# A conv block on one core: one tile's copies moved behind a sigmoid, four subtractions moved from VectorE to POOL

## The chip, the cores and the metric

The kernel runs on one core of one Trainium2 chip. The metric is the device time of one execution in microseconds (us), as a median of several runs. Engines are named as in the profile: PE (TensorE, matmuls) with PEld (its weight loads), DVE (VectorE), ACT (ScalarE), POOL (GpSimd) and SP (SyncE, which here only issues DMAs).

## The reference

One decoder layer on 256 tokens of width 2048, in float32, with a modulation by a condition vector `c`. The layer's mixer is a gated depthwise convolution of 31 taps; the attention mixers of the reference are not used at depth 1.

```python
mod = silu(c) @ mod_w + mod_b
sh1, sc1, g1, sh2, sc2, g2 = split(mod, 6)
h = rms_norm(x, norm1_g) * (1 + sc1) + sh1
a, gt = split(h @ conv_w_in + conv_b_in, 2)
u = a * sigmoid(gt)
u = causal_depthwise_conv(u, conv_dw_w, 31 taps) + conv_dw_b
u = silu(layer_norm(u, conv_ln_g, conv_ln_b))
y = u @ conv_w_out + conv_b_out
x = x + (1 + g1) * y
h = rms_norm(x, norm2_g) * (1 + sc2) + sh2
u = square(relu(h @ mlp_w1))
x = x + (1 + g2) * (u @ mlp_w2)
```

## The kernel before

**Tiles.** Activations lie with channels on the 128 partitions: 16 channel tiles of 128 x 256 tokens. Weights come from HBM as tiles of 1 MB (128 x 2048, `raw`, five buffers, loaded in the order of a written list by SP). To keep float32 accuracy, each weights tile is split in two halves of 128 x 1024, and each half into a high part and a low part: `hi` is a copy by ACT (L203), `lo` is the difference `raw - hi` by VectorE or POOL (L206). Both have six buffers. PE multiplies hi and lo with the split activations (`hl`, `u2`).

**Stages, in order of time.**

1. Start (to about 138 us): the modulation's columns are formed on VectorE (L381, one multiply and sum over 128 x 2048 for each 1 MB column tile `mod_c`), the first norm is made, and PE multiplies the first eight pairs of the input projection in plain float32 into eight held accumulators (L550).
2. Input projection, jobs 8 to 15: each job has two weights tiles, `("in", i, 0)` for `a` and `("in", i, 1)` for the gate. The result goes through `evac` (L506, L507) and `gate` (a sigmoid on ACT, L738, and a product on VectorE, L740) into `u[i]`. Beside it run the convolutions. Eight channel tiles are convolved on VectorE, tap by tap (L609 to L618). The other eight (`PE_TILES`) go to PE (L723): for these ACT or VectorE first makes sixteen shifted copies of `u[i]` into a tile `wide` (`copy_wide`, L700), and POOL makes a diagonal matrix (L708). `COPY_AT` tells at which job the copies of which tile are put: at job 8 those of tile 0. PE also multiplies the remaining modulation rows (L307) between the jobs.
3. The first `gate` calls are for the eight held accumulators, `held[0]` to `held[7]`. They share the code place with the split of job 8's two weights tiles:

```python
split_w(jobs[HELD] + (0,), nc.gpsimd)
with tc.issue_after(state["w_hi"]):
    gate(0, held[0])
for i in range(1, 6):
    gate(i, held[i])
with tc.issue_after(state["sg"].ins):
    split_w(jobs[HELD] + (1,), nc.gpsimd)
with tc.issue_after(state["w_hi"]):
    gate(6, held[6])
gate(7, held[7])
```

4. Layer norm of the convolved tiles (from about 300 us), with silu.
5. Output projection, eight pairs `("out", 0)` to `("out", 7)` (about 309 to 411 us). The prediction calls these jobs 0 to 7 of the output stage. Each has two weights tiles, so four halves to split; a pair's result is scaled by ACT (L904) and added to the residual `x` by VectorE (L905), then ACT squares it (L907), POOL sums the squares into `sqacc` (L909, L912), and ACT and VectorE split the scaled result (L916, L214, L217). Sixteen more columns of the modulation are formed on VectorE beside it (L381).
6. The MLP in four quarters (to the end).

**Order.** A scheduler sorts each engine's instructions by priorities and by a planned time of its own; `urgent()` raises a priority, and `tc.issue_after(x)` puts what is inside behind the instruction `x`. Each engine then works off its own list in that order. `state["sg"]` is the sigmoid of the last `gate` call made so far.

**Who makes the low parts.** All of the input projection's are made by POOL (but for one half of job 8). For the pairs in the list `POOLED` they are made by POOL as well; all other pairs' are made by VectorE.

## Time and profile before

| What | us |
|---|---|
| Median of 3 runs | 1118.45 |
| Lowest and highest run | 1117.72, 1119.9 |
| The profiled execution, its own time | 1120.38 |
| Span of the profiled execution, first to last instruction | 1118.6 |
| PE busy in that span | 1092.7 |
| DVE, ACT, POOL busy | 761.7, 506.6, 164.9 |

The profile is of one execution. A row of its timeline has start and duration in us, engine, line, operation, output and inputs by the program's names, partitions x elements, how many instructions are merged, and in brackets the engine's idle time before it and what ended it. A table of stretches has, for each engine, its busy time in the stretch, then the clock that was granted to PE as a share of full speed, the share of time that the DMA engines were busy, and what they moved.

### The profile page before, as it was taken

The page shows a single profiled execution, that of the slowest core. Times are in us where ns is not written, and L with a number is a line of the kernel's source. Part 1 is how long each engine was busy: PE and PEld are TensorE (multiplying, and loading weights), DVE is VectorE, ACT ScalarE, POOL GpSimd, SP SyncE. Part 2 cuts the span into 40 slices and gives each one's busy share as a digit, 9 for nine tenths or more (in the row PEclk, how much of TensorE's full clock was granted, in tenths as well). Part 3 has the DMA queues.
Part 4 walks back from the last instruction along what each step waited for, and adds up shares of the span by engine and source line. Part 5 has one row for each costly group of instructions (what it writes and reads, how often), then busy time and mean ns, then how long its engine had stood idle before and what let it go on. Part 6 is the DMA issues. An engine that isn't in the chain of part 4 may idle for free.

```text
span 1118.6 us, 15367 instructions
## 1 busy us (share of the span) xinstructions
PE 1092.7 (98%) x6018; PEld 897.3 (80%) x6018; DVE 761.7 (68%) x1018; ACT 506.6 (45%) x675; POOL 164.9 (15%) x102
## 2 busy tenths in 40 slices
PE   7999989999999999999999999999999999999998
PEld 4887856766789988888888888888888888888887
DVE  5777679798399977676776567644656566565553
ACT  4111284673566568444344444334444433444441
POOL 0000175657443434000000000000000000000000
PEclk8999989999999989999999999999999999999999
DMA  9999977998489977798898889758788877788641
GB/s 384 420 421 421 416 283 308 406 326 309 145 345 358 387 252 264 233 285 268 337 368 310 249 235 305 271 180 260 229 249 240 230 207 223 217 253 248 212 142 38
DMA packets 142314, 314.22 MB, mean 281 GB/s; under 512 B 87585, under 2 KB 105505, under 8 KB 107297
## 3 DMA queue, kind: packets, MB, share of 16 engines
q1 hardware_dynamic: 142096, 313.11, 80.7%
q8 instruction: 47, 0.77, 0.3%
q14 instruction: 25, 0.20, 0.0%
q10 hardware_dynamic: 146, 0.13, 0.0%
HBM read 301.15 MB, written 12.07 MB: 280 GB/s over the span
## 4 chain that ended last, share of the span: by engine, by line
PE 78%; DMA 12%; DVE 6%; ACT 2%; issue 2%; POOL 1%; ACTq 0%; SPq 0%; POOLq 0%; DVEq 0%
PE mm L255 20%; PE mm L254 20%; PE mm L256 20%; DMA raw<-mod_c 8%; PE mm L231 4%; PE mm L227 3%; PE mm L229 3%; PE mm L228 2%; DVE raw L381 2%; DMA raw<-w_in 2%; PE mm L232 2%; DVE acc L615 2%; PE row L307 1%; DMA raw<-w_out 1%; ACT wide L700 1%
## 5 line engine op out<-in xcount | busy, mean ns | idle before, releaser
L203 ACT ACTIVATE hi<-raw 128x1024 fp32r<-128x1024 f32 x320 | 334.7, 1057 | 371.7 <-PE mm L256 297.3
L206 DVE TENSOR_TENSOR lo<-raw,hi 128x1024 fp32r<-128x1024 f32 x273 | 335.7, 1238 | 175.3 <-ACT hi L203 173.2
L255 PE MATMUL mm<-lo,u 128*128 128x512 f32 x496 | 193.1, 389 | 0.0
L254 PE MATMUL mm<-hi,u 128*128 128x512 f32 x496 | 193.0, 389 | 0.0
L256 PE MATMUL mm<-hi,u 128*128 128x512 f32 x496 | 192.9, 389 | 0.0
L254 PE MATMUL mm<-hi,hl 128*128 128x512 f32 x480 | 186.7, 389 | 0.0
L256 PE MATMUL mm<-hi,hl 128*128 128x512 f32 x480 | 186.7, 389 | 0.0
L255 PE MATMUL mm<-lo,hl 128*128 128x512 f32 x480 | 186.7, 389 | 0.0
L381 DVE SCALAR_TENSOR_TENSOR raw<-raw,cond 128x2048 f32<-128x2048 f32 x62 | 146.1, 2363 | 50.5 <-DMA raw<-mod_c 50.3
L206 POOL TENSOR_TENSOR lo<-raw,hi 128x1024 fp32r<-128x1024 f32 x47 | 114.5, 2459 | 216.0 <-DMA raw<-w_in 132.4
L256 PEld LDWEIGHTS mm<-hi,u 128*128 128x128 f32 x496 | 93.1, 188 | 19.4
L255 PEld LDWEIGHTS mm<-lo,u 128*128 128x128 f32 x496 | 93.1, 188 | 19.3 <-DVE lo L206 0.4
L254 PEld LDWEIGHTS mm<-hi,u 128*128 128x128 f32 x496 | 93.1, 188 | 19.0
L256 PEld LDWEIGHTS mm<-hi,hl 128*128 128x128 f32 x480 | 90.1, 188 | 18.8
L254 PEld LDWEIGHTS mm<-hi,hl 128*128 128x128 f32 x480 | 90.1, 188 | 18.7
L255 PEld LDWEIGHTS mm<-lo,hl 128*128 128x128 f32 x480 | 90.1, 188 | 18.6
L615 DVE SCALAR_TENSOR_TENSOR acc<-u,v,acc 128x256 f32<-128x256 f32 x224 | 94.6, 488 | 1.8
L227 PE MATMUL mm<-hl,hi 128*128 128x256 f32 x288 | 82.7, 289 | 4.4 <-ACT hi L203 2.2
L231 PE MATMUL mm<-hl,hi 128*128 128x512 f32 x224 | 83.7, 412 | 3.0 <-ACT hi L203 2.2
L229 PE MATMUL mm<-hl,lo 128*128 128x256 f32 x288 | 82.8, 288 | 0.6 <-DVE lo L206 0.6
L228 PE MATMUL mm<-hl,hi 128*128 128x256 f32 x288 | 82.7, 288 | 0.2 <-DVE hl L217 0.2
L550 PE MATMUL mm<-two,first 128*128 128x256 f32 x256 | 60.7, 392 | 8.5 <-ACT two L581 8.5
(170 smaller groups left out, 1193.9 us busy)
## 6 DMA issues: line engine op xcount, KB each, us to landing
raw<-w SPq DMA_DIRECT2D x128, 1024.0 KB, 5.3
raw<-mod_c SPq DMA_DIRECT2D x62, 1024.0 KB, 9.2
raw<-mod_r SPq DMA_DIRECT2D x32, 1024.0 KB, 7.7
raw<-w_in SPq DMA_DIRECT2D x16, 1024.0 KB, 6.9
raw<-w_out SPq DMA_DIRECT2D x16, 1024.0 KB, 6.4
first<-w_first SPq DMA_DIRECT2D x15, 1024.0 KB, 17.2
flat<-two SPq DMA_DIRECT2D x30, 256.0 KB, 2.7
two<-flat SPq DMA_DIRECT2D x120, 64.0 KB, 4.3
```

Source lines behind the costliest of these rows:

```text
L203: state["w_hi"] = nc.scalar.activation(hi, w[:, ks, :], AF.Copy).ins
L206: end = by.tensor_tensor(lo, w[:, ks, :], hi.bitcast(F32), op=ALU.subtract)
L227: nc.tensor.matmul(out_p, w, m[:, 0:T], start=begin, stop=False)
L228: nc.tensor.matmul(out_p, w, m[:, T : 2 * T], start=False, stop=False)
L229: state["mm_end"] = nc.tensor.matmul(out_p, lo[:, k % HALF, :], m[:, 0:T], start=False, stop=end)
L231: nc.tensor.matmul(p[:, c, :], hi[:, k % HALF, :], m, start=(k == 0), stop=(k == KT - 1))
L254: nc.tensor.matmul(p, p_hi, hi, start=begin, stop=False)
L255: nc.tensor.matmul(p, p_hi, lo, start=False, stop=False)
L256: nc.tensor.matmul(p, p_lo, hi, start=False, stop=end)
L381: nc.vector.scalar_tensor_tensor(w, w, 1.0, cb, op0=ALU.mult, op1=ALU.mult, accum_out=acc)
L550: step = nc.tensor.matmul(held[n][:, c, :], w[:, 2 * n + c, :], h, start=k == 0 and c == 0, stop=k == KT - 1, skip_group_check=True)
L615: nc.vector.scalar_tensor_tensor(out, s, w, acc, op0=ALU.mult, op1=ALU.add)
```

## The change

Two edits. In the list of pairs whose low parts are made by POOL, `("out", 2)` is added. And the call that makes the shifted copies of tile 0 (at job 8, which equals `HELD`) is put inside `issue_after`, behind the sigmoid of the last `gate` call, that of `held[7]`; the other calls of `copy_wide` stay as they are.

```diff
-POOLED = [("out", 0), ("out", 1), ("up", 0, 1), ("up", 0, 2)]
+POOLED = [("out", 0), ("out", 1), ("out", 2), ("up", 0, 1), ("up", 0, 2)]
...
         if n in COPY_AT:
-            copy_wide(COPY_AT[n], False)
+            with tc.issue_after(state["sg"].ins) if n == HELD else ExitStack():
+                copy_wide(COPY_AT[n], False)
```

Both edits also move other instructions, since the scheduler plans anew. In the changed program's lists: ACT has sigmoids 3 to 5 and the hi halves of job 8's second tile ahead of all copies of tile 0; ten of the copies come after sigmoid 7, then the hi halves of job 9's first tile, then the last six. Further on, the two instructions that make the shift of the convolution (L658) stand ahead of the four hi halves of job 12 instead of between them. In the output stage POOL has four lows of `("out", 2)` between those of `("out", 1)` and the first sum of squares, and VectorE's L905 of pair 0 comes directly after an L381, no longer behind three of these lows. SP issues the same loads in the same order; some of them wait for a slot that POOL frees where it was VectorE or PE before.

## The prediction

> **What bounds the kernel now.** I read the page of the profile first (busy shares, the granted clock in slices, the chain), then tables of busy time by stretch.

> ```profile
> PE 1092.7 (98%) x6018; PEld 897.3 (80%) x6018; DVE 761.7 (68%) x1018; ACT 506.6 (45%) x675; POOL 164.9 (15%) x102
> PEclk8999989999999989999999999999999999999999
> PE 78%; DMA 12%; DVE 6%; ACT 2%; issue 2%; POOL 1%; ACTq 0%; SPq 0%; POOLq 0%; DVEq 0%
> 440.00:1118.00 678.00, 674.75 (x3021) 560.11 (x3019) 421.97 (x445) 279.10 (x286) 0.25 (x1) 1.00 0.77 242
> ```

> PE is busy 98% of the span and makes 78% of the chain. From 440 us on it has 674.75 of 678 us busy at full clock, so whatever PE gains or loses before 440 comes out at the end unchanged. The question is where PE stands still or runs slowly before 440. The clock line has two tenths under 9 there, the sixth and the fifteenth slice (about 140 to 168 and 391 to 420 us). Narrow stretches (PE alone) show both places, and a third for comparison:

> ```profile
> 143.09:146.50 3.41, 0.72 (x3) 1.00 0.35 147
> 146.50:153.33 6.83, 5.42 (x16) 0.50 0.32 95
> 306.93:310.35 3.42, 1.95 (x18) 1.00 1.04 441
> 392.26:395.68 3.42, 1.25 (x11) 1.00 0.97 376
> 395.68:402.50 6.82, 6.27 (x28) 0.50 0.92 315
> ```

> Columns: stretch, length, busy PE, granted clock, DMA share. At 143 us PE is idle 2.69 us of 3.41, then gets half clock for 6.83 us. At 392 us it is idle 2.17 us of 3.42, again with half clock for 6.82 us behind. At 307 us it is idle 1.47 us and the clock stays. So in this trace an idle share between 1.47 and 2.17 us of such a stretch is where the penalty begins. [...]

> The change touches the first place and the stage ahead of the second.

> **Edit 1, the copies behind the last sigmoid.** ACT, then PE and POOL, then the load concerned and PE's last matmuls of the held groups:

> ```profile
> 135.12 0.84 ACT L738 ACTIVATE two<-mm,v 128x256 f32<-128x256 f32 x2 [0.56 <-DVE u L740]
> 137.85 5.40 ACT L700 ACTIVATE wide<-u 32x284 f32<-32x284 f32 x12 [1.89 <-issue]
> 143.65 0.83 ACT L738 ACTIVATE two<-acc,v 128x256 f32<-128x256 f32 x2
> 144.36 2.01 ACT L203 ACTIVATE hi<-raw 128x1024 fp32r<-128x1024 f32 x2
> 145.47 0.49 PE L231 MATMUL mm<-hl,hi 128*128 128x512 f32 x1 [2.16 <-ACT hi L203]
> 147.91 0.58 PE L232 MATMUL mm<-hl,lo 128*128 128x256 f32 x1 [1.94 <-POOL lo L206]
> 145.50 14.07 POOL L206 TENSOR_TENSOR lo<-raw,hi 128x1024 fp32r<-128x1024 f32 x6 [7.25 <-ACT hi L203]
> 124.64 2.88 SPq L184 DMA_DIRECT2D raw<-w_in  x3
> raw<-w_in SPq DMA_DIRECT2D x1, 1024.0 KB, 11.5
> 134.15 1.89 PE L550 MATMUL acc<-two,first 128*128 128x256 f32 x8
> 136.74 1.03 PE L550 MATMUL row<-two,first 128*128 128x256 f32 x4
> 137.41 0.59 PE L231 MATMUL mm<-hl,hi 128*128 128x512 f32 x1
> 143.04 0.28 PE L232 MATMUL mm<-hl,lo 128*128 128x256 f32 x1
> ```

> After three sigmoids ACT's queue holds twelve copies of the shifted tile. They wait until PE has finished the start stage (137.77) and then run to 143.25. Queued behind them are the sigmoids 3 to 7 and the two hi halves of job 8's second weights tile, whose load had landed at 124.64 + 11.5 = 136.1. PE waits 2.16 us for that hi, 1.94 us for its low part on POOL.

> In the changed program's order ACT has sigmoids 3 to 5 next, then the two hi halves, sigmoids 6 and 7, and only then copies. Acc's matmuls end at 136.04, so three sigmoids at 0.42 us (0.84 for two) end by about 137.8 even if the first waits for VectorE's last gate product. The hi halves (2.01 for two) end by 138.9 and 139.8, and POOL's lows, 14.07 / 6 = 2.35 us each, at about 141.3 and 143.7. PE comes to them at 143.3 and needs the second half three us later: no wait, with 2 us to spare. Gained: idle 2.69 + (6.83 - 5.42) = 4.10 us, and half of the 5.42 us at half clock, 2.71. Together 6.8 us.

> What comes late next? The copies move behind: ten from about 141, then the hi halves of job 9's first tile to 147.5, its lows at 149.0 and 151.4. PE took 5.9 us for job 8's first tile (137.41 to 143.32), so it ends the second near 149; a group of row matmuls lies between, so job 9 starts about 150 with its first low there. The next tile's lows are due 154.1 and 156.5, ahead of PE by 3 us. The copies themselves feed a convolution that PE begins only after job 9. Loads on SP's queue wait for slots that POOL's lows and PE's row matmuls free; both come earlier, and the DMA engines have room:

> ```profile
> 143.50:154.30 10.80, 6.88 (x25) 4.65 (x25) 10.52 (x27) 10.65 (x19) 8.80 (x4) 0.68 0.36 125
> 211.28 0.88 DVE L613 SCALAR_TENSOR_TENSOR acc<-u,v,small 128x256 f32<-128x256 f32 x2 [8.04 <-ACT shift L658]
> 239.28 0.47 PE L231 MATMUL mm<-hl,hi 128*128 128x512 f32 x1 [0.56 <-DVE u L740]
> ```

> The DMA share is 0.36 there. VectorE's taps could have taken the gain back later, since PE waits 0.56 us for VectorE at 239. But VectorE itself had stood 8.04 us waiting for ACT's shift, and the new order puts both shift instructions ahead of four hi halves that stood before or between them. I take the 0.56 us as gone too. Edit 1: -7.4 us. Its bounds: -4.1 if only the idle time comes back, -8 if PE's later small waits shrink as well.

> **Edit 2, third output pair's lows on POOL.** Rows of VectorE, POOL, PE and ACT in the output stage:

> ```profile
> 322.16 4.25 DVE L381 SCALAR_TENSOR_TENSOR raw<-raw,cond 128x2048 f32<-128x2048 f32 x1
> 326.40 3.35 DVE L206 TENSOR_TENSOR lo<-raw,hi 128x1024 fp32r<-128x1024 f32 x1
> 330.17 2.29 DVE L381 SCALAR_TENSOR_TENSOR raw<-raw,cond 128x2048 f32<-128x2048 f32 x1
> 332.46 2.35 DVE L206 TENSOR_TENSOR lo<-raw,hi 128x1024 fp32r<-128x1024 f32 x2
> 334.80 0.68 DVE L905 TENSOR_TENSOR x<-mm,x 128x512 f32<-128x512 f32 x1
> 321.85 6.82 POOL L206 TENSOR_TENSOR lo<-raw,hi 128x1024 fp32r<-128x1024 f32 x2 [7.22 <-ACT hi L203]
> 335.54 0.38 PE L227 MATMUL mm<-hl,hi 128*128 128x256 f32 x1 [0.87 <-DVE x L905]
> 338.00:390.00 52.00, 52.00 (x436) 52.00 (x435) 51.35 (x48) 30.05 (x46) 17.15 (x11) 1.00 0.98 375
> 380.46 2.35 DVE L206 TENSOR_TENSOR lo<-raw,hi 128x1024 fp32r<-128x1024 f32 x2
> 370.39 1.11 ACT L904 ACTIVATE mm<-mm,gb,modc 128x256 f32<-128x256 f32 x2 [1.04 <-PE mm L229]
> 381.91 0.54 ACT L904 ACTIVATE mm<-mm,gb,modc 128x256 f32<-128x256 f32 x1 [3.38 <-PE mm L229]
> 393.42 1.11 ACT L904 ACTIVATE mm<-mm,gb,modc 128x256 f32<-128x256 f32 x2 [4.81 <-PE mm L229]
> 394.46 1.99 ACT L203 ACTIVATE hi<-raw 128x1024 fp32r<-128x1024 f32 x2
> 395.55 0.49 PE L227 MATMUL mm<-hl,hi 128*128 128x256 f32 x1 [2.17 <-ACT hi L203]
> ```

> From 338 to 390 both PE (52.00) and VectorE (51.35) are full. VectorE looks like the engine to relieve, but the first rows speak against it. While POOL makes two lows (321.85 to 328.67), VectorE's L381 takes 4.25 us instead of 2.29 and its low 3.35 instead of 1.17 (2.35 for two); POOL's two take 6.82 instead of 4.7. The two engines take turns: whoever waits goes next. [...]

> VectorE saves four lows, 4 x 1.17 = 4.7 us. It pays POOL's four holds: (6.82 - 2.2) / 2 = 2.3 each, 9.2. Some of that is covered: L905 (0.68, one operand in PSUM) can run under a hold, twice, 1.4; and the 2.2 us that the low at 326.40 waited now falls on an L381 that arrives about 0.8 later. Sum 9.2 - 4.7 - 1.4 - 0.8 = +2.3 us for VectorE. Bounds: -4.7 if no hold is felt, +4.5 if all are.

> What does PE feel? Jobs take 11.5 us (L904 at 370.39, 381.91, 393.42). L905 stands earlier in the new order, so PE's wait of 0.87 at 335.54 goes, and PE reaches job 6 at 381.0 instead of 381.9 (times before edit 1's shift). Its first low was ready at 380.46 + 1.17 = 381.6, only just in time; with 2.3 more it is ready at 383.9. PE starts job 6 2.0 us later than before. POOL's own lows, alternating with L381s from 330.9, end about 333, 337.5, 340.3 and 343.7, where job 2 needs them from 334.6 every 2.9 us: up to 0.5 us late, which is contained in the later wait. Two loads wait on POOL instead of VectorE and go out some us later; VectorE takes them up later still. Behind the four lows on POOL stand the sums of squares, which nobody needs before job 7 ends. Job 7's wait (2.17 us) stays, because ACT's order still has both L904 of job 6 ahead of that hi. Edit 2: +2.0 us, bounds 0 (a gain is excluded by job 7's wait, which nothing in edit 2 touches, except for the 0.87) and +4.2.

> **The sum.** -7.4 + 2.0 = -5.4 us. The profiled execution took 1120.38 us (span 1118.6, 1.8 around it), 1.9 above the median of 1118.45. From the profiled one it is 1115.0; from the median, 1113.0 us.

> **Rivals.**
> *A new half clock.* PE's wait at job 6 is 383.9 - 381.0 = 2.9 us, less what earlier waits took out of it. If over about 2 us of it fall into one stretch of 3.41, PE runs 6.8 us at half clock, +3.1 (half of 6.27): 1116.1 us. For it: 2.17 us were enough at 392. Against: the wait may be cut in two by the grid or be spread over jobs 2, 5 and 6. [...]
> *The old half clock lapses.* Job 7's idle 2.17 us lay wholly in one stretch; moved by 5 us it may straddle two, -3.1: 1109.9 us.
> [...]
> *No net change.* Edit 1 brings back only the idle 4.1 us (job 9's tiles late in turn), edit 2 costs its bound of 4.2: 1118.5 us. The order does change as said, so "nothing happens" needs this balance.

> **How the numbers follow.** About 0.2% (2.2 us) can be told from no change. Forecast 1113.0: 0.42. New half clock 1116.1, at the edge of that: 0.19, two thirds of it faster. Old half clock lapses: 0.14. No net change: 0.08. Slower: 0.17. Faster 0.42 + 0.14 + 0.13 = 0.69, same 0.06 + 0.08 = 0.14, slower 0.17. The range runs from 1109 (the lapse) to 1118.5 (no net change), leaving out mainly the slower case.

> **What would show it.** Right: no PE gap between 143 and 150, full clock there, ACT's twelve copies after 140; L658 before the hi pair; POOL's L206 of the output stage stretched to over 3 us each and L381 beside them to over 4; a wait of PE at L229 on VectorE's low about two jobs before the end of the output stage. Wrong: PE waiting for job 9's hi or low; VectorE's L381 at 2.3 us beside POOL's lows; PE waiting on POOL's low in job 2.

## The result, and the profile after

| Kernel | Median, us | Lowest to highest, us | Runs |
|---|---|---|---|
| before | 1118.42 | 1117.35 to 1119.9 | 5 |
| changed | 1113.38 | 1112.88 to 1114.59 | 5 |

The ratio is 0.9956, with a 95% interval from 0.9942 to 0.9971: faster by 5.0 us, where 5.4 was forecast. The profiled execution took 1112.88 us (span 1110.9). Lines behind 772 have numbers one higher than before: L904 is now L905, and L905 is L906.

First the page of the changed kernel: busy time and the granted clock in slices.

```profile
PE 1087.3 (98%) x6018; PEld 893.0 (80%) x6018; DVE 767.9 (69%) x1014; ACT 506.7 (46%) x675; POOL 176.6 (16%) x106
PEclk8999999999999999999999999999999999999999
```

PE is busy 5.4 us less (1092.7 before) with the same 6018 matmuls. That is time at half clock which is gone (half of 5.42 and of 6.27 would be 5.8): the two slices below 9 are no longer in the clock line. VectorE is busy 6.2 us more, although it has four instructions fewer.

Now the stretches of the prediction (PE alone, except in the last row, which has all engines):

```profile
143.09:146.50 3.41, 3.41 (x21) 1.00 0.83 283
146.50:153.33 6.83, 6.83 (x42) 1.00 0.45 154
386.17:389.58 3.41, 1.89 (x16) 1.00 0.99 389
389.58:393.00 3.42, 2.01 (x14) 1.00 0.95 388
432.00:1110.00 678.00, 675.07 (x3022) 560.33 (x3020) 422.62 (x446) 280.25 (x288) 0.70 (x1) 1.00 0.77 242
```

The first place is full at full clock. At the second (job 7 of the output stage) PE still stands idle, but 1.52 us of it lie in one stretch and 1.41 in the next, and no half clock follows. (These two stretches are steps of 3.413 us, counted from 24.35 us, where this trace's only earlier half clock ends.) From there on nothing changed: 675.07 us of 678 are busy, 674.75 before.

The start of the input projection, ACT and POOL:

```profile
137.81 2.01 ACT L203 ACTIVATE hi<-raw 128x1024 fp32r<-128x1024 f32 x2
140.42 4.51 ACT L700 ACTIVATE wide<-u 32x284 f32<-32x284 f32 x10
138.95 4.77 POOL L206 TENSOR_TENSOR lo<-raw,hi 128x1024 fp32r<-128x1024 f32 x2 [0.42 <-ACT hi L203]
146.09 4.76 POOL L206 TENSOR_TENSOR lo<-raw,hi 128x1024 fp32r<-128x1024 f32 x2 [2.37 <-ACT hi L203]
196.85 0.36 ACT L658 ACTIVATE small<-small 128x256 f32<-128x256 f32 x1
```

Job 8's hi halves are ready at 139.82 instead of 146.37, the ten copies follow at 140.42, and the lows of jobs 8 and 9 come ahead of PE: from 137 us to the output stage PE no longer waits for ACT or POOL. L658, for whose result VectorE had stood 8.04 us, runs at 196.85.

The output stage: VectorE, POOL and PE's waits, and below them PE's first matmul of that stage in the kernel before.

```profile
314.54 4.24 DVE L381 SCALAR_TENSOR_TENSOR raw<-raw,cond 128x2048 f32<-128x2048 f32 x1
323.14 0.68 DVE L906 TENSOR_TENSOR x<-mm,x 128x512 f32<-128x512 f32 x1
324.18 3.45 DVE L381 SCALAR_TENSOR_TENSOR raw<-raw,cond 128x2048 f32<-128x2048 f32 x1 [0.37 <-DMA raw<-mod_c]
327.56 2.89 DVE L217 TENSOR_TENSOR u<-two,u 128x512 fp32r<-128x512 f32 x1
330.37 6.76 DVE L206 TENSOR_TENSOR lo<-raw,hi 128x1024 fp32r<-128x1024 f32 x2
343.22 0.68 DVE L217 TENSOR_TENSOR u<-two,u 128x512 fp32r<-128x512 f32 x1
314.23 21.82 POOL L206 TENSOR_TENSOR lo<-raw,hi 128x1024 fp32r<-128x1024 f32 x6 [7.26 <-ACT hi L203]
375.25 2.35 DVE L206 TENSOR_TENSOR lo<-raw,hi 128x1024 fp32r<-128x1024 f32 x2
302.14 0.50 PE L227 MATMUL mm<-hl,hi 128*128 128x256 f32 x2 [1.41 <-ACT hl L214]
363.06 0.39 PE L229 MATMUL mm<-hl,lo 128*128 128x256 f32 x1 [0.78 <-DVE lo L206]
376.52 0.39 PE L229 MATMUL mm<-hl,lo 128*128 128x256 f32 x1 [1.69 <-DVE lo L206]
390.23 0.38 PE L227 MATMUL mm<-hl,hi 128*128 128x256 f32 x1 [2.17 <-ACT hi L203]
```

```profile
309.77 0.50 PE L227 MATMUL mm<-hl,hi 128*128 128x256 f32 x2 [1.40 <-ACT hl L214]
```

POOL's six lows take 3.64 us each (about 2.4 alone, by the fence above). Beside them VectorE's L381 takes up to 4.24 us, two lows 6.76 instead of 2.35, and L217 2.89, where it takes 0.68 at 343.22 with nothing on POOL. The residual add L906 ran in 0.68 us at 323.14, beside one of them. The first L381 stands beside the second pair's lows and is no longer than before (4.25); what edit 2 adds are the rows from 324.18 on. PE pays later: 0.78 us at job 5, 1.69 us at job 6, both for VectorE's lows. The wait of 0.87 us for L905 is gone.

### The profile page after: what moved, and what is told of

It is laid out like the page before. It is cut to its first block, busy times and chain, and to the rows that moved or that the text cites. A ratio compares the mean times of both kernels' runs of the same rounds, so it can differ in the third digit from the quotient of the medians.

```text
span 1110.9 us, 15369 instructions
## 1 busy us (share of the span) xinstructions
PE 1087.3 (98%) x6018; PEld 893.0 (80%) x6018; DVE 767.9 (69%) x1014; ACT 506.7 (46%) x675; POOL 176.6 (16%) x106
## 4 chain that ended last, share of the span: by engine, by line
PE 80%; DMA 10%; DVE 5%; issue 2%; POOL 2%; ACT 1%; SPq 0%; DVEq 0%; POOLq 0%; ACTq 0%
PE mm L255 20%; PE mm L254 20%; PE mm L256 20%; DMA raw<-mod_c 8%; PE mm L231 6%; PE mm L232 3%; DVE raw L381 3%; PE row L307 2%; PE mm L723 2%; DMA raw<-w_out 1%; POOL lo L206 1%; DVE lo L206 1%; PE mm L228 1%; PE mm L229 1%; PE mm L227 1%
## 5 line engine op out<-in xcount | busy, mean ns | idle before, releaser
L203 ACT ACTIVATE hi<-raw 128x1024 fp32r<-128x1024 f32 x320 | 334.2, 1058 | 355.6 <-PE mm L256 301.0
L206 DVE TENSOR_TENSOR lo<-raw,hi 128x1024 fp32r<-128x1024 f32 x269 | 332.7, 1246 | 173.0 <-ACT hi L203 172.5
L381 DVE SCALAR_TENSOR_TENSOR raw<-raw,cond 128x2048 f32<-128x2048 f32 x62 | 147.1, 2374 | 47.6 <-DMA raw<-mod_c 47.5
L206 POOL TENSOR_TENSOR lo<-raw,hi 128x1024 fp32r<-128x1024 f32 x51 | 130.7, 2591 | 205.1 <-ACT hi L203 205.1
L229 PE MATMUL mm<-hl,lo 128*128 128x256 f32 x288 | 81.8, 284 | 3.4 <-DVE lo L206 3.2
L227 PE MATMUL mm<-hl,hi 128*128 128x256 f32 x288 | 81.2, 284 | 3.6 <-ACT hi L203 2.2
L231 PE MATMUL mm<-hl,hi 128*128 128x512 f32 x224 | 81.9, 406 | 0.0
L228 PE MATMUL mm<-hl,hi 128*128 128x256 f32 x288 | 81.6, 284 | 0.2 <-DVE hl L217 0.2
L550 PE MATMUL mm<-two,first 128*128 128x256 f32 x256 | 60.6, 391 | 8.4 <-ACT two L581 8.4
## 6 DMA issues: line engine op xcount, KB each, us to landing
raw<-w SPq DMA_DIRECT2D x128, 1024.0 KB, 5.4
raw<-mod_c SPq DMA_DIRECT2D x62, 1024.0 KB, 9.2
raw<-mod_r SPq DMA_DIRECT2D x32, 1024.0 KB, 7.7
raw<-w_in SPq DMA_DIRECT2D x16, 1024.0 KB, 7.0
raw<-w_out SPq DMA_DIRECT2D x16, 1024.0 KB, 7.0
first<-w_first SPq DMA_DIRECT2D x15, 1024.0 KB, 17.1
```

The source lines that it names most:

```text
L203: state["w_hi"] = nc.scalar.activation(hi, w[:, ks, :], AF.Copy).ins
L206: end = by.tensor_tensor(lo, w[:, ks, :], hi.bitcast(F32), op=ALU.subtract)
L227: nc.tensor.matmul(out_p, w, m[:, 0:T], start=begin, stop=False)
L228: nc.tensor.matmul(out_p, w, m[:, T : 2 * T], start=False, stop=False)
L229: state["mm_end"] = nc.tensor.matmul(out_p, lo[:, k % HALF, :], m[:, 0:T], start=False, stop=end)
L231: nc.tensor.matmul(p[:, c, :], hi[:, k % HALF, :], m, start=(k == 0), stop=(k == KT - 1))
```

## The experiments

All ratios are to the kernel before, run on the same chip beside it, with 95% intervals. The kernels' line numbers shift by one to four where code was added.

**Edit 1 alone.**

```diff
-POOLED = [("out", 0), ("out", 1), ("out", 2), ("up", 0, 1), ("up", 0, 2)]
+POOLED = [("out", 0), ("out", 1), ("up", 0, 1), ("up", 0, 2)]
```

(against the changed kernel)

> Edit 1 alone (the low parts of the third output pair stay on VectorE). My theory: the whole gain is edit 1's, 7.4 to 7.9 us, from PE's idle time and half clock at 143 us; so 1111.0 us against 1118.4 before, and about 2 us faster than the changed kernel. In the trace no PE gap and full clock at 143 us, VectorE's L381 beside POOL's two remaining lows still over 4 us, PE's gap of 0.87 us on VectorE's L905 back, no gap on VectorE's lows before job 7. Rival: part of the changed kernel's gain is edit 2's (VectorE relieved); then this one is slower than the changed kernel, 1115 us or more.

Measured: 1112.85 us (1110.23 to 1114.01), ratio 0.9938 (0.9924 to 0.9952). The median is only 0.5 us below the changed kernel's, but the five runs fall into two groups: 1110.23 and 1110.46 at a mean granted clock of 0.998, and 1112.85, 1112.91 and 1114.01 at 0.992. So the executions of one program differ by 2.4 us or more, and the slower ones had the lower clock. The profiled one, of the first group, shows in its page and in stretches of PE a half clock behind an idle stretch:

```profile
PE 1087.7 (98%) x6018; PEld 894.0 (81%) x6018; DVE 765.6 (69%) x1018; ACT 506.5 (46%) x675; POOL 162.4 (15%) x102
299.07:302.48 3.41, 1.80 (x16) 1.00 1.09 461
302.48:305.89 3.41, 3.41 (x18) 0.50 0.97 413
301.47 0.50 PE L227 MATMUL mm<-hl,hi 128*128 128x256 f32 x2 [1.39 <-ACT hl L214]
328.11 0.39 PE L227 MATMUL mm<-hl,hi 128*128 128x256 f32 x1 [0.48 <-DVE x L906]
388.13 0.39 PE L227 MATMUL mm<-hl,hi 128*128 128x256 f32 x1 [2.17 <-ACT hi L203]
```

The wait of 1.39 us before the output stage, which cost only itself in the kernel before, was followed by 3.41 us of half clock here, with 1.61 us idle in its stretch. From the first matmul of the output stage to the first of job 7 it is 388.13 - 301.47 = 86.66 us, less half of 3.41 is 84.95. In the changed kernel the same way is 390.23 - 302.14 = 88.09 at full clock. In these two traces edit 2 on top of edit 1 thus costs 3.1 us. By the ratios (0.9956 and 0.9938) it is some 2 us, with intervals that overlap. VectorE's busy time is 765.6 us: edit 2 adds 2.3 to it although it takes four lows of 1.17 us off, so its other work takes 7.0 us more. The wait for the residual add (L905 before, L906 here) came back as expected, with 0.48 us for 0.87.

**Edit 2 alone.**

```diff
-POOLED = [("out", 0), ("out", 1), ("up", 0, 1), ("up", 0, 2)]
+POOLED = [("out", 0), ("out", 1), ("out", 2), ("up", 0, 1), ("up", 0, 2)]
```

> Edit 2 alone (the copies of tile 0 stay ahead of the sigmoids). [...] Rival: VectorE, 51 of 52 us busy there, is relieved of 4.7 us, and the kernel gains 1 to 3 us: 1116 to 1117 us.

Measured: 1122.13 us (1121.13 to 1124.59), ratio 1.0028 (1.0018 to 1.0038). Slower, by some 3 us; 1120.4 us was expected, with VectorE 2.3 us behind, and up to 1123.5 with a new half clock. PE's wait and the stretches around it:

```profile
309.12 0.50 PE L227 MATMUL mm<-hl,hi 128*128 128x256 f32 x2 [1.39 <-ACT hl L214]
383.43 0.43 PE L229 MATMUL mm<-hl,lo 128*128 128x256 f32 x1 [2.69 <-DVE lo L206]
398.62 0.39 PE L227 MATMUL mm<-hl,hi 128*128 128x256 f32 x1 [2.17 <-ACT hi L203]
380.22:383.63 3.41, 0.71 (x6) 1.00 0.98 382
383.63:387.04 3.41, 3.41 (x17) 0.50 0.98 394
```

Here the whole wait falls on job 6, 2.69 us in one piece, and the new half clock comes, 3.41 us long. The way to job 7 is 398.62 - 309.12 = 89.50 us against 395.55 - 309.77 = 85.78 before: +3.7, of which 1.7 is the half clock and 2.0 is left for the waits.

**Edit 1's place filled instead of emptied.** The kernel before, with four useless float32 matmuls in the gap at job 8. ACT's order is the same up to 190 us; later the scheduler sorts some of it anew.

```diff
             for c in range(2) if i < KT - 1 else (1, 0):
+                if n == HELD and c == 1:
+                    for _ in range(4):
+                        nc.tensor.matmul(p[:, 1, :], ones, cond[:, 0:4, :], start=True, stop=True)
```

> The kernel before with four matmuls of no use (float32, 128x128 by 128x512, written to the place that the next real matmul starts anew) put between job 8's two weights tiles, where PE otherwise stands idle. They take PE about 3.5 us, so the idle time is no shorter for the real work. My theory, that 2.7 of the 6.8 us at 143 us are half clock after an idle stretch: full clock stays, 2.7 us faster, 1115.7 us. Rival: only the wait itself counts, and the time stays at 1118.4 us.

Measured: 1117.53 us (1115.81 to 1119.67), ratio 0.9985 (0.9976 to 0.9994).

```profile
143.00:146.40 3.40, 3.40 (x12) 1.00 0.41 166
307.71:311.12 3.41, 3.41 (x19) 0.50 0.97 416
147.97 0.39 PE L232 MATMUL mm<-hl,lo 128*128 128x256 f32 x1 [0.94 <-POOL lo L206]
150.95 1.07 PE L307 MATMUL row<-raw,cz 128*32 128x512 f32 x8
532.73 0.50 PE L255 MATMUL mm<-lo,u 128*128 128x512 f32 x1 [0.93 <-DVE lo L206]
```

With work that nobody needs in the gap the half clock does not come: the next stretch, 146.40 to 149.80, has a granted clock of 1.00. POOL's low holds PE until the same moment (147.97, 147.91 before), but PE comes to the row matmuls behind job 8 at 150.95 instead of 153.33, 2.4 us earlier. ACT had the same order there, so this part of edit 1's gain is the clock's. The whole kernel gained 1.7 us (0.7 to 2.7 by the interval) rather than 2.7. A half clock at 307.71 and a wait of 0.93 us at 532.73, which the kernel before hasn't, cost some of it, and the new order on ACT behind 190 us changed other waits, so the median does not give the size of this part.

**Who pays: the subtractions left out.** Pool writes zeros and reads nothing in the third pair.

```diff
-                end = by.tensor_tensor(lo, w[:, ks, :], hi.bitcast(F32), op=ALU.subtract)
+                if key[:2] == ("out", 2):
+                    end = nc.gpsimd.memset(lo.bitcast(F32), 0.0)
+                else:
+                    end = by.tensor_tensor(lo, w[:, ks, :], hi.bitcast(F32), op=ALU.subtract)
```

(against the changed kernel)

> The changed kernel, but Pool writes zeros into the third output pair's low parts and reads nothing (the subtractions of that pair are left out of the computation). It parts the work saved on VectorE from the price of Pool's reads. [...] Rival (VectorE's operations are slow there because of DMA traffic or the order, not because of Pool's reads): L381 and L217 stay slow, the waits of 0.78 and 1.69 us stay, 1113.4 us.

Measured: 1111.51 us (1110.62 to 1114.46), ratio 0.9943 (0.9927 to 0.9958). From 1111 to 1112.9 us was expected if POOL's subtractions make VectorE slow there. L384, L220, L209 and L230 are L381, L217, L206 and L227 of the changed kernel.

```profile
PE 1088.9 (98%) x6018; PEld 895.7 (81%) x6018; DVE 758.7 (68%) x1014; ACT 505.9 (46%) x675; POOL 165.4 (15%) x106
320.19 3.63 POOL L207 MEMSET lo<- 128x1024 f32 x4
323.04 2.29 DVE L384 SCALAR_TENSOR_TENSOR raw<-raw,cond 128x2048 f32<-128x2048 f32 x1
325.25 1.22 DVE L220 TENSOR_TENSOR u<-two,u 128x512 fp32r<-128x512 f32 x1
327.87 2.36 DVE L209 TENSOR_TENSOR lo<-raw,hi 128x1024 fp32r<-128x1024 f32 x2 [1.40 <-ACT hi L203]
301.36 0.50 PE L230 MATMUL mm<-hl,hi 128*128 128x256 f32 x2 [1.39 <-ACT hl L217]
386.03 0.44 PE L230 MATMUL mm<-hl,hi 128*128 128x256 f32 x1 [2.17 <-ACT hi L203]
```

Both kernels have the same 1014 instructions on VectorE, and the changed one's total is 767.9 - 758.7 = 9.2 us higher. Not all of that is the price of POOL's four subtractions. The four instructions of VectorE that ran beside them (L381, L217 and two lows, from 324.18 on) take 3.45 + 2.89 + 6.76 = 13.10 us in the changed kernel and 2.29 + 1.22 + 2.36 = 5.87 here: 7.2 us. The other 2.0 us lie outside these rows, where both kernels give POOL the same work. The way to job 7 is 386.03 - 301.36 = 84.67 us, 3.4 shorter, and PE's waits at jobs 5 and 6 are gone. The rival, that DMA traffic or the order made VectorE slow there, falls: the third column operation is back at 2.29 us. It began while POOL still wrote its zeros (until 323.82); the instructions after it had nothing of the third pair beside them. So the run shows that POOL's subtractions are the cause. That it is their reading rests on two rows: L384 took 2.93 us at 319.48, beside the last of POOL's earlier subtractions (until 320.2) and then the zeros, and 2.29 at 323.04.

**Twice the dose.** The changed kernel with the fourth pair on POOL as well.

```diff
-POOLED = [("out", 0), ("out", 1), ("out", 2), ("up", 0, 1), ("up", 0, 2)]
+POOLED = [("out", 0), ("out", 1), ("out", 2), ("out", 3), ("up", 0, 1), ("up", 0, 2)]
```

> The changed kernel with the low parts of the fourth output pair on Pool too: twice the dose of the second edit. The theory that a low part on Pool holds VectorE up while both read: VectorE loses another 2 to 2.5 us net and TensorE, which waits 0.78 and 1.69 us for low parts in the changed kernel already, waits for it in full: about 1115.7 us, and 1117.4 us if the longer idle sets a half clock at job 6 as it did with the second edit alone. Rival (VectorE is relieved of 4.7 us a pair, and what the second edit lost is a matter of the order of the third pair alone): TensorE's waits at job 6 get shorter, 1111 to 1112 us.

Measured: 1118.2 us (1117.18 to 1123.25), ratio 0.9997 (0.9984 to 1.0011). All of edit 1's gain is used up.

```profile
346.94 0.39 PE L229 MATMUL mm<-hl,lo 128*128 128x256 f32 x1 [1.18 <-POOL lo L206]
351.91 0.39 PE L229 MATMUL mm<-hl,lo 128*128 128x256 f32 x1 [1.83 <-POOL lo L206]
379.88 0.39 PE L229 MATMUL mm<-hl,lo 128*128 128x256 f32 x1 [1.69 <-DVE lo L206]
```

The time was near what was expected, the mechanism not: PE now waits for POOL's own lows as well, 1.18 and 1.83 us, while the wait for VectorE at job 6 stays at 1.69. With eight lows of the third and fourth pair to make, and two sums of squares between them, POOL falls behind PE.

**Half a dose less.** Edit 1, and the second pair's second tile back on VectorE.

```diff
-POOLED = [("out", 0), ("out", 1), ("out", 2), ("up", 0, 1), ("up", 0, 2)]
+POOLED = [("out", 0), ("up", 0, 1), ("up", 0, 2)]
```

(The lines are against the changed kernel. The second pair's first tile doesn't change hands by this: POOL has 100 instructions, two fewer than in edit 1 alone.)

> The first edit alone, and the low parts of the second output pair's second tile on VectorE as well (half a dose less than the kernel before). [...] Rival (Pool's help is worth what it takes off VectorE): VectorE is 4.7 us later, TensorE waits for lows at job 6: 1115 to 1117 us.

Measured: 1110.46 us (1107.67 to 1111.7), ratio 0.9924 (0.9909 to 0.9939).

```profile
314.06 2.28 DVE L381 SCALAR_TENSOR_TENSOR raw<-raw,cond 128x2048 f32<-128x2048 f32 x1
385.49 0.54 ACT L905 ACTIVATE mm<-mm,gb,modc 128x256 f32<-128x256 f32 x1 [4.88 <-PE mm L229]
387.05 0.38 PE L227 MATMUL mm<-hl,hi 128*128 128x256 f32 x1 [1.60 <-ACT hi L203]
```

L381 is back at 2.28 us, and no wait for a low is left ahead of job 7. From 1111.5 to 1112.9 us was expected, with L381 back at about 2.3 us; it was better by 1 us. Part of that is the order of ACT, which came out with only one L905 instead of two ahead of job 7's hi and shortened the wait from 2.17 to 1.60 us; the rest is not explained.

**Job 7's hi halves first.** Edit 1, and job 6's two scalings on ACT behind the hi halves of job 7's first tile.

```diff
+                if key == ("out", HALF - 1, 0):
+                    state["hi_7"] = state["w_hi"]
...
-                    nc.scalar.activation(t2[:, c, :], t2[:, c, :], AF.Identity, scale=mcol(G1, k), bias=gb[:, k : k + 1])
+                    with tc.issue_after(state["hi_7"]) if i == HALF - 2 else ExitStack():
+                        nc.scalar.activation(t2[:, c, :], t2[:, c, :], AF.Identity, scale=mcol(G1, k), bias=gb[:, k : k + 1])
```

> Edit 1 alone, and the scaling of job 6's result (L904) put behind the hi halves of job 7's first weights tile on ACT. My theory of job 7's wait: it is made by ACT's order, since the load had landed before; PE's 2.17 us go, and VectorE's last L381, which ended 0.9 us before the low could start, is the next bound. Between 0.9 and 2.7 us faster than edit 1 alone: 1108.3 to 1110.1 us; if a half clock stood behind that wait in the run compared, 3 us more. Rival: the load or VectorE sets that moment, and the time is edit 1's.

Measured: 1110.83 us (1109.45 to 1113.0), ratio 0.9924 (0.9911 to 0.9938). ACT, VectorE (L383 and L208 are L381 and L206) and PE:

```profile
381.99 2.01 ACT L203 ACTIVATE hi<-raw 128x1024 fp32r<-128x1024 f32 x2 [2.40 <-DMA raw<-w_out]
385.08 2.28 DVE L383 SCALAR_TENSOR_TENSOR raw<-raw,cond 128x2048 f32<-128x2048 f32 x1
387.30 2.35 DVE L208 TENSOR_TENSOR lo<-raw,hi 128x1024 fp32r<-128x1024 f32 x2
388.57 0.39 PE L231 MATMUL mm<-hl,lo 128*128 128x256 f32 x1 [2.28 <-DVE lo L208]
```

The wait for the hi is gone and one of 2.28 us for the low stands in its place: the hi was ready at 384.0, but VectorE had a column operation ahead of the low. A half clock of 3.41 us follows (389.71 to 393.12, behind a step with 2.27 us of idle time), and the time came out 0.7 us above the expected range.

**And a column operation one job later**, added to the last.

```diff
-LATE_OUT = [1, 2, 2, 3, 3, 3, 1, 1]
+LATE_OUT = [1, 2, 2, 3, 3, 2, 2, 1]
```

> The first edit alone, the scaling of job 6 behind the high halves of job 7's first tile as in the run before, and one of the column operations of VectorE that stood ahead of job 7's first low parts moved one job later. Theory: the 2.28 us that TensorE waited for VectorE at job 7 with the high halves first goes, since the lows start one operation of 2.28 us earlier, and with it the half clock there: 1108.3 to 1109.5 us. Rival (VectorE is late by more than one operation, or a half clock arises at another idle stretch): 1110 to 1111 us, the time of the high halves first.

Measured: 1109.72 us (1108.72 to 1110.63), ratio 0.9921 (0.9908 to 0.9934). The wait at job 7 is gone, as expected; a smaller one, of 1.23 us, stands behind the stage at 406.75. A wait near the stage's start, which the run before had as well (1.76 us at 328.20), is followed by a half clock here:

```profile
328.17 0.38 PE L229 MATMUL mm<-hl,hi 128*128 128x256 f32 x1 [1.77 <-DVE x L909]
329.62:333.03 3.41, 3.41 (x19) 0.50 1.06 380
```

**Both**: this kernel with half a dose less.

```diff
-POOLED = [("out", 0), ("out", 1), ("up", 0, 1), ("up", 0, 2)]
+POOLED = [("out", 0), ("up", 0, 1), ("up", 0, 2)]
```

> The run with the column moved later, and the second output pair's second low parts back on VectorE as in the run with fewer lows. [...] Rival (the two edits take the same wait away, or VectorE's lows now hold the later tiles up): 1109.7 to 1110.5 us, as each alone.

Measured: 1106.8 us (1106.43 to 1107.42), ratio 0.9888 (0.9872 to 0.9905), the fastest of all. From 1106.3 to 1108.5 us was expected if the wait at 328 us goes, and the half clock behind it. All engines in the stretch around job 7:

```profile
380.00:400.00 20.00, 20.00 (x159) 19.55 (x158) 17.36 (x18) 13.68 (x20) 6.61 (x4) 1.00 0.88 338
```

PE has no idle time left at job 7; its next wait is 1.16 us at 404.08. The wait at 328 us is gone too, so the two edits did not take the same wait away.

## Why the prediction was right

**Edit 1, -7.4.** PE's waits at 145.47, 147.91 and 239.28 went, and ACT's and POOL's times came within 0.6 us of those worked out (hi ready at 139.82 against 139.8, lows at 143.72 against 143.7, copies from 140.42 against 141). Before the output stage the changed kernel is 309.77 - 302.14 = 7.6 us earlier. Copies that now stand ahead of job 9's hi halves held nobody up: no wait ended by ACT or POOL is left there. Of the 2.7 us put down to the clock, 2.4 came back where the gap was filled instead.

**Edit 2, +2.0.** The way from the output stage's first matmul to job 7 took 88.09 us against 85.78: +2.3. The step that carried it, POOL's holds, held: 9.2 us less 1.4 under cover, 7.8, was the price set down for them, and 7.2 us is what VectorE's four instructions beside them gave back with the subtractions left out. Of the two residual adds in the 1.4, one ran beside POOL's lows, in 0.68 us at 323.14; the other came at 337.06, when POOL had finished them. (The 9.2 us by which VectorE's totals differ agrees with the 9.2 of the sum by chance.) Counted from the stage's first matmul, VectorE started the first low of job 6 at 375.25 - 302.14 = 73.1 us instead of 380.46 - 309.77 = 70.7: 2.4 us late, where 2.3 was forecast. The low of job 6 was forecast for 383.9, which is 376.3 with 7.6 of edit 1 taken off; it was ready at 375.25 + 1.17 = 376.4. PE's wait of 2.9 us came as 0.78 + 1.69 = 2.47 in two pieces. Against edit 1 alone edit 2 costs 3.1 us, so the change was faster by its first edit only. Beside POOL's subtractions L217 took 2.89 us instead of 0.68, while L384, begun as POOL wrote zeros, took 2.29. POOL's lows were drawn out too, to 3.64 us each on average (4.48 at most) instead of 2.4.

**The rivals.** The new half clock at job 6 did not come in the changed kernel, where 0.78 us of waiting lay at job 5 and 1.69 at job 6; with edit 2 alone it came, but half as long as priced (3.41 us, so 1.7 instead of 3.1). The slower case (0.17) did not come: in the changed kernel's output stage PE waited for none of POOL's lows. With twice the dose it did, 1.18 and 1.83 us. "No net change" falls with edit 1's ratio of 0.9938. The old half clock did lapse in the profiled execution: job 7's idle lay in two stretches. The span fell by 1118.6 - 1110.9 = 7.7 us; with 7.6 from edit 1 and 2.3 against it from edit 2, 2.4 are left for the lapse, of the 3.1 priced.

**The step that was not sound: from the profiled execution to the median.** From one profiled execution to the other the time fell by 1120.38 - 1112.88 = 7.5 us, not by 5.4, because the half clock at job 7, which the sum kept, lapsed. The prediction set the sum against the profiled execution, with half clocks in full, and then took 1.9 us off to come to the median. But half clocks differ from run to run. Among seventeen runs of the kernel before on one chip, five with a mean granted clock of 0.997 or 0.998 took 1116.53 to 1118.15 us and eleven with 0.989 to 0.991 took 1119.3 to 1122.67 (one had 0.994). The profiled execution had 0.991. So runs of one kernel differ in how much half clock they had. Where they had it the mean doesn't say: it also counts 6.82 us of half clock at 16.80 in the profiled execution, and the changed kernel's trace has as much there (17.52 to 24.35). It is likely, not shown, that the half of 5.42 us that edit 1 gives back, and the half clock at job 7, are in some runs and not in others. The five runs of the changed kernel all have 0.996 to 0.998. That the forecast of 1113.0 came within 0.4 us of 1113.38 is therefore partly luck, with two uncounted terms in it: in part of the runs of before there was less half clock to gain, and the changed kernel seems to lose less at job 7 than was kept in the sum. That these cancel is an estimate from the mean clocks; the runs that were only timed have no trace to show it.

## What to carry to other kernels

An engine that is full need not be helped by moving work to another: price what the two cost each other from the rows where both run (here 7.2 us for four against 4.7 saved), and try the move in the other direction as well: here it was part of the fastest version. When a wait is taken away, look at once for the one behind it: job 7's wait passed from ACT's hi to VectorE's low, and with both gone a wait for a residual add near the stage's start was still followed by a half clock (3.41 us); the edits together were the fastest. And when a half clock comes in some executions and not in others, look at the granted clock of the runs before reading a difference of medians below 3 us.

## What the runs showed of the hardware

```profile
384.40:387.81 3.41, 1.56 (x14) 1.00 0.95 320
```

PE's work in the step did not prevent the half clock: 0.71 us in the step at 380.22 of edit 2 alone, 1.80 us in the one at 299.07 of edit 1 alone. What decides between 1.52 and 2.12 us stays open.
